# An attention stage whose softmax, weight conversion and matmuls are put in another order

## The chip, the cores and the metric

One core of a Trainium2 chip runs the whole kernel. A core has TensorE (PE: matmuls; PEld in the profile is its weight load), VectorE (DVE), ScalarE (ACT), GpSimd (POOL) and SyncE (SP, whose queue issues most DMAs). Each engine works through its own instructions in order and waits for others by semaphores. The time is that of one execution on the device in microseconds (us), the median of several.

## The reference

A trunk of two layers over 256 tokens of width 1024, all in float32. The stage that is edited is the attention of layer 1: three head groups of eight heads of 64, each with its own causal window and dilation; keys and values `k_sh`, `v_sh` are computed before.

```python
q = apply_rope((h @ w_q).reshape(B, S, N_ATTN_GROUPS, HEADS_PER_GROUP, HEAD_DIM), cos, sin)
for g, (window, dilation) in enumerate(ATTN_GROUPS):     # per group
    s = einsum(q, k) * Dh ** -0.5;  s = where(mask, s, NEG_BIG)
    m = max(s);  p = exp(s - m);  den = sum(p)
    o = einsum(p / den, v);  lse = m + log(den)
wts = softmax(stack(lses), axis=0)                       # over the groups
o = sum(wts[..., None] * stack(outs), axis=0)
return o.reshape(B, S, O_WIDTH) @ w_o
```

Weighting the groups by their `lse` and adding them is one softmax over the keys of all three groups together, which is how the kernel does it. After the mixer come a post norm, the residual sum, a pre norm and a SwiGLU feed-forward.

## The kernel before

**Numbers in two parts.** For matmuls each float32 weight is split: `hl[:, 0]` is the weight rounded to a shorter form (the high part, a copy on ScalarE, L99), `hl[:, 1]` what is left (the low part, a subtraction on VectorE, L100). Activations are split alike. A product is three matmuls (`proj_mm`, `row_mm`): high by high, high by low, low by high. Weights come by DMA in blocks into three raw buffers (`rawp`) and are converted into `hl` buffers (six, and two more called `xy`). A DMA waits on SP's queue until the block that had its raw buffer is converted.

**Tiles.** The tokens are two halves of 128 (`i` = 0, 1). The heads are eight in each group, two at a time: four pairs (`pr` = 0 to 3), with all three groups of the pair together, 384 query columns. So there are eight half tiles `(pr, i)`.

**A half tile** takes these steps:
- `q_proj`: 24 matmuls into a PSUM bank `qp`, in two halves of 12, with weights of `load_q_units`.
- `rope` (the rotation): four VectorE instructions (L658 to L662, `ra_q`, `rb_q`).
- `q_turn`: three transposes on PE into `qtp`, copied by ScalarE to `qT` (L772).
- `scores`: 12 matmuls into two PSUM banks `sc` (one for each head, `e` = 0, 1); VectorE adds the mask and takes the row maximum (L710), multiplies it by -0.125 (`nm`, L712), ScalarE takes the exponential and its row sum `den` (L714).
- `over_sums`: VectorE's reciprocal (L720), and GpSimd's multiplication of the weights `p` by it (L721).
- `p_turn`: eight transposes on PE into `ptp`, two ScalarE copies (L737).
- `values`: 16 matmuls into `ob`; ScalarE and VectorE split the result into the parts of `oT` (L748, L749).

**The tail.** `o_proj(i, chunks)` multiplies `oT` by the output weights, one of four chunks for each pair, into two banks `acc_o` of each half. `go.first` is the post norm with the residual sum, `go.second` the pre norm, `go.third` the transposes `tp_m` into the next input `aT`; `go(1, ...)` does all three for half 1. The next feed-forward opens with the matmuls `acc_b`, whose first four converted blocks it takes from `first_units` if there are any, or loads.

**What sets the order.** The kernel's tool decides the order of instructions on each engine by itself, except within `manual_schedule`, where the engines that it names go in the order in which the code is written. In the loop over pairs that holds for PE, VectorE and ScalarE, in the tail for PE alone. PSUM banks are handed round: four for `qp`, `sc` and `acc_o`, two (`gu`) for `qtp`, `ob` and the last scores, two for `ptp` and `tp_m`; a step waits until the user of its bank before has been read.

Of the kernel before, what the change touches and what calls it, by code (L numbers as in the profile page):

```python
# [19 lines left out]
P = 128  # L20
# [27 lines left out]
def trunk_kernel(ctx: ExitStack, tc: tile.TileContext, x, pos, gains, pscale, ws, wq, invf, amask, pmat, icnt, out):  # L48
# [72 lines left out]
    def load_q_units(pr, b):  # L121
        raw = rawp.tile([P, 2, 1024], F32, tag="raw", name=f"rawq{pr}{b}")
        nc.sync.dma_start(raw[:, :, :768], wq[pr * 2 + b])
        return [parts(raw, k, 768, pr % 2 == 0 and b == 0) for k in range(2)]
# [564 lines left out]
    qT = [qx[g // 2][:, g % 2].rearrange("p (r s) -> p r s", r=4) for g in range(3)]  # L689
    am = qx[2][:, 0].bitcast(BF16).rearrange("p (i k) -> p i k", i=2)  # L690
    pTt = [t.rearrange("p (c t) -> p c t", c=4) for t in (qx[1][:, 1, 0:512], qx[1][:, 1, 512:1024], qx[2][:, 1])]
    nc.gpsimd.dma_start(am, amask.rearrange("i p k -> p i k"))
    npt = [0]
    probs = {}

    def scores(pr, i, pool=accp, tag="acc"):
# [3 lines left out]
        sc = [pool.tile([P, 512], F32, tag=tag, name=f"sc{i}_{pr}{e}") for e in range(2)]  # L700
        for o, g, keys in ((0, 0, slice(0, S)), (256, 1, t), (384, 2, t)):
            for e in range(2):
                a = slice(e * 64, e * 64 + 64)
                n = keys.stop - keys.start
                mm(sc[e][:, o : o + n], q[g][a, t], kT[g][a, pr, keys], True, True)
        probs[i, pr] = []
        for e in range(2):
            p = sc2.tile([P, 512], F32, tag="w2", name=f"p{i}_{pr}{e}")
            mx = st.tile([P, 1], F32, tag="mx", name=f"mx{i}_{pr}{e}")
            nc.vector.tensor_tensor_reduce(p, sc[e], am[:, i], 1.0, -3.0e38, op0=ALU.add, op1=ALU.max, accum_out=mx)  # L710
            nm = st.tile([P, 1], F32, tag="nm", name=f"nm{i}_{pr}{e}")
            nc.vector.tensor_scalar_mul(nm, mx, -0.125)  # L712
            den = st.tile([P, 1], F32, tag="den", name=f"den{i}_{pr}{e}")
            nc.scalar.activation(p, p, AF.Exp, bias=nm, scale=0.125, accum_out=den)  # L714
            probs[i, pr].append((p, den))

    def over_sums(pr, i):
        for e, (p, den) in enumerate(probs[i, pr]):
            rd = st.tile([P, 1], F32, tag="rd", name=f"rd{i}_{pr}{e}")
            nc.vector.reciprocal(rd, den)  # L720
            nc.gpsimd.tensor_scalar_mul(p, p, rd)  # L721
            probs[i, pr][e] = p

    oT = [None, None]

    pT = {}

    def p_turn(pr, i):

        pT[i, pr] = []  # L730
        for e in range(2):
            tp = tpp.tile([P, 4, P], F32, tag="tp", name=f"ptp{i}_{pr}{e}")
            for c in range(4):
                nc.tensor.transpose(tp[:, c], probs[i, pr][e][:, c * P : (c + 1) * P], ident)
            pT[i, pr].append(pTt[npt[0] % len(pTt)])
            npt[0] += 1
            nc.scalar.copy(pT[i, pr][e], tp)  # L737

    def values(pr, i):
# [4 lines left out]
        for c, (g, j) in enumerate(((0, 0), (0, 1), (1, i), (2, i))):  # L744
            for e in range(2):
                n = slice((2 * pr + e) * 64, (2 * pr + e) * 64 + 64)
                mm(ob[e * 64 : e * 64 + 64, 0:P], vt[g][:, j, n], pT[i, pr][e][:, c], c == 0, c == 3)
# [3 lines left out]
    acc_f = [None, None]  # L751

    def o_proj(i, chunks):
# [5 lines left out]
    def q_proj(pr, i, half, units):  # L759
# [4 lines left out]
        if half == 1:  # L764
            qr[pr, i] = rope(qp[i][:, :384], i, 6, f"q{pr}{i}")

    def q_turn(pr, i):
# [3 lines left out]
        for g in range(3):  # L771
            nc.scalar.copy(qT[g][:, pr, i * P : (i + 1) * P], tp[:, g])  # L772

    qp, qr = {}, {}
    units = []

    def next_q(pr, k):

        if k % 2 == 0:
            units.extend(load_q_units(pr + 1, k // 2) if pr < 3 else load_units(2))  # L780

    with tc.manual_schedule(engines={mybir.EngineType.PE}):
        with tc.manual_schedule(engines={mybir.EngineType.DVE, mybir.EngineType.Activation}):
# [178 lines left out]
```

## Time and profile before

| | |
|---|---|
| median of 3 runs (lowest, highest) | 984.6 us (982.15, 986.87) |
| the profiled execution, its span | 985.76 us, 984.0 us |
| mean granted clock of PE | 0.986 |
| busy: PE, PEld, VectorE, ScalarE, GpSimd | 950.4, 783.7, 684.1, 542.9, 62.3 us |
| first query matmul of the stage | 699.35 us |
| first matmul of the output projection | 767.43 us |
| gate matmuls of the last feed-forward run on from | 794.77 us |

The span runs from the first to the last instruction; the execution's time is some 2 us longer. Matmuls overlap at their ends, so paces are read from start to start. A row of the trace's order of time has the start, the length, the engine, the line, the operation with what it writes and reads, how many were merged, and in brackets how long the engine had waited before it and for whom. The "granted clock" is the share of PE's full clock.

### The profile page before, as it was taken

What the parts mean: (1) busy time and instruction counts of PE and PEld (TensorE: products, weight loads), DVE (VectorE), ACT (ScalarE), POOL (GpSimd) and SP (SyncE); (2) the same over time, 40 slices, a digit from 0 to 9 for tenths busy, and PEclk for the clock granted to TensorE, in tenths of its full rate; (3) what the DMA queues carried; (4) which work ended last, traced back from release to release, by engine and by line L of the source; (5) the groups of instructions that cost most, each with busy time, mean ns of one, the idle gap of its engine ahead of it and who ended that gap; (6) DMA issues with size and microseconds to landing.
All of it is one profiled execution on the core that took longest, in us unless ns stands there. A gap on an engine that the chain in (4) does not pass through costs nothing.

```text
span 984.0 us, 12092 instructions
## 1 busy us (share of the span) xinstructions
PE 950.4 (97%) x4560; PEld 783.7 (80%) x4560; DVE 684.1 (70%) x771; ACT 542.9 (55%) x693; POOL 62.3 (6%) x66
## 2 busy tenths in 40 slices
PE   7999999999999999999999999999987899999997
PEld 6888788878788878877888888788976778887886
DVE  5979874577788886458887964785465587887642
ACT  6665753455657565347656743644345576665531
POOL 0000000000100000000000000100033310000000
PEclk8999999999999999999999999999999799999999
DMA  7886876475468687546687765564324236967721
GB/s 248 286 266 205 259 260 207 173 227 187 164 211 265 181 280 261 179 139 213 153 317 218 268 243 175 177 217 139 127 95 153 86 107 194 330 163 260 247 90 43
DMA packets 55898, 197.16 MB, mean 200 GB/s; under 512 B 7392, under 2 KB 7392, under 8 KB 53792
## 3 DMA queue, kind: packets, MB, share of 16 engines
q1 hardware_dynamic: 53456, 179.35, 52.2%
q0 software_dynamic: 2384, 17.04, 8.9%
q8 instruction: 36, 0.59, 0.2%
q14 instruction: 22, 0.18, 0.0%
HBM read 178.54 MB, written 1.05 MB: 183 GB/s over the span
## 4 chain that ended last, share of the span: by engine, by line
PE 74%; DVE 11%; ACT 5%; DMA 4%; issue 3%; POOL 2%; SPq 0%; POOLq 0%; DVEq 0%; ACTq 0%
PE acc_d L127 22%; PE g L127 12%; PE st L314 12%; PE u L127 7%; PE acc_b L127 6%; PE vp L127 3%; DVE hl L100 3%; PE kp L127 3%; DMA xy<-raw 2%; DVE hl_lo L107 2%; PE htp L295 2%; ACT hl L99 2%; PE qp L127 1%; DVE h L193 1%; PE acc_w L127 1%
## 5 line engine op out<-in xcount | busy, mean ns | idle before, releaser
L100 DVE TENSOR_TENSOR hl<-raw,hl 128x1024 fp32r<-128x1024 f32 x182 | 221.0, 1222 | 111.6 <-ACT hl L99 110.5
L99 ACT CAST hl<-raw 128x1024 fp32r<-128x1024 f32 x182 | 189.7, 1051 | 138.3 <-PE acc_d L127 103.3
L127 PE MATMUL acc_d<-hl,h 128*128 128x512 f32 x1056 | 243.5, 390 | 0.0
L127 PEld LDWEIGHTS acc_d<-hl,h 128*128 128x128 f32 x1056 | 197.3, 188 | 40.4
L107 DVE TENSOR_TENSOR hl_lo<-xy,hl_hi 128x2048 fp32r<-128x2048 f32 x40 | 91.6, 2291 | 48.6 <-ACT hl_hi L106 48.6
L107 DVE TENSOR_TENSOR hl_lo<-raw,hl_hi 128x2048 fp32r<-128x2048 f32 x48 | 109.4, 2285 | 15.6 <-ACT hl_hi L106 15.5
L106 ACT CAST hl_hi<-xy 128x2048 fp32r<-128x2048 f32 x40 | 76.5, 1913 | 64.0 <-DVE xy L333 29.7
L106 ACT CAST hl_hi<-raw 128x2048 fp32r<-128x2048 f32 x48 | 91.9, 1914 | 20.8 <-PE st L314 10.6
L127 PE MATMUL acc_b<-hl,aT_m 128*128 128x512 f32 x192 | 44.8, 392 | 0.3 <-ACT aT_m L205 0.3
L127 PEld LDWEIGHTS acc_b<-hl,aT_m 128*128 128x128 f32 x192 | 35.7, 188 | 8.3 <-ACT aT_m L205 0.8
L127 PE MATMUL g<-hl_hi,aT_m 128*128 128x512 f32 x128 | 41.9, 393 | 0.0
L127 PE MATMUL u<-hl_hi,aT_m 128*128 128x512 f32 x128 | 41.8, 393 | 0.0
L314 PE MATMUL st<-hl_hi,S_m 128*128 128x512 f32 x128 | 41.8, 393 | 0.0
L127 PE MATMUL qp<-hl,aT_f 128*128 128x384 f32 x192 | 38.9, 354 | 0.0
L297 ACT CAST h<-htp 128x512 fp32r<-128x512 f32 (+1 forms) x48 | 26.2, 548 | 20.0 <-PE htp L295 20.0
L127 PEld LDWEIGHTS qp<-hl,aT_f 128*128 128x128 f32 x192 | 34.8, 198 | 1.3 <-issue 0.8
L127 PE MATMUL kp<-hl,aT_hk 128*128 128x512 f32 x144 | 34.6, 394 | 0.0
L331 POOL DMA_DIRECT2D xy<-raw x16 | 14.1, 878 | 305.2 <-DVE xy L333 82.3
L127 PE MATMUL vp<-hl,aT_hk 128*128 128x512 f32 x144 | 33.1, 390 | 0.0
L314 PE MATMUL st<-hl_hi,aT_m 128*128 128x512 f32 x96 | 31.6, 393 | 1.3 <-ACT hl L99 0.9
L721 POOL TENSOR_SCALAR p<-p,rd 128x512 f32<-128x512 f32 x16 | 24.9, 1566 | 121.9 <-DVE rd L720 100.1
L298 DVE TENSOR_TENSOR h<-htp,h 128x512 fp32r<-128x512 f32 (+1 forms) x48 | 30.6, 640 | 1.1 <-ACT h L297 1.0
(246 smaller groups left out, 1596.4 us busy)
## 6 DMA issues: line engine op xcount, KB each, us to landing
raw<-in_ws SPq DMA_DIRECT2D x278, 512.0 KB, 4.8
xy<-in_ws SPq DMA_DIRECT2D x32, 512.0 KB, 6.8
xy<-raw POOLq DMA_DIRECT2D x16, 1024.0 KB, 8.1
rawq<-in_wq SPq DMA_DIRECT2D x8, 768.0 KB, 4.7
gain_post<-in_gains SPq DMA_DIRECT2D x14, 256.0 KB, 5.0
gain_pre<-in_gains SPq DMA_DIRECT2D x12, 256.0 KB, 6.1
rawpm<-in_pmat SPq DMA_DIRECT2D x2, 512.0 KB, 4.1
out_dram<-h SPq DMA_DIRECT2D x4, 256.0 KB, 2.1
```

What stands on the lines that cost most here:

```text
L99: nc.scalar.copy(hl[:, 0, :n], raw[:, k, :n])
L100: last["dve"] = nc.vector.tensor_sub(hl[:, 1, :n], raw[:, k, :n], hl[:, 0, :n])
L106: nc.scalar.copy(hi, raw)
L107: last["dve"] = nc.vector.tensor_sub(lo, raw, hi)
L127: nc.tensor.matmul(o, l, r, start=start, stop=stop)
L193: nc.vector.scalar_tensor_tensor(h[i][:, c], y[:, c], rs, h[i][:, c], op0=ALU.mult, op1=ALU.add)
L295: nc.tensor.transpose(tp[:, k], prod[c, i][:, k * P : (k + 1) * P], ident)
L297: nc.scalar.copy(d[:, 0], tp[:, :nt])
L298: nc.vector.tensor_sub(d[:, 1], tp[:, :nt], d[:, 0])
L314: nc.tensor.matmul(ps, a(z, k), u[v], start=start and k == 0 and n == 0, stop=k == 3 and n == 2, skip_group_check=not start,)
L331: nc.gpsimd.dma_start(dst, src, accum_op=ALU.add)
L721: nc.gpsimd.tensor_scalar_mul(p, p, rd)
```

## The change

The loop's steps are written anew in half-tile steps. One function, `between`, stands after each half tile's query matmuls. It does the high parts of one block of weights, issues the next block's DMA, then the rotation of this half tile, scores and masks of the half tile before (`new`), the transposes and copies of the softmax weights of the one before that (`old`), with the exponentials around the copies, then the low parts, and last the division by the sums. Transposes of the queries and value matmuls stand between the two halves of the next 12 query matmuls. Besides:
- the weights `p` are divided by their sums on VectorE, not on GpSimd;
- the mask instruction scales by -0.125 and takes the minimum, so the separate small multiplication goes;
- three query copies become two; the buffers of turned softmax weights are two, not three;
- blocks of output weights go through `between` too (`b` = 8, 9), and two blocks of first gate weights are converted by hand in the tail;
- the tail's order is written anew, and holds for VectorE and ScalarE as well.

```diff
-            nc.vector.tensor_tensor_reduce(p, sc[e], am[:, i], 1.0, -3.0e38, op0=ALU.add, op1=ALU.max, accum_out=mx)
-            nc.vector.tensor_scalar_mul(nm, mx, -0.125)
-            nc.scalar.activation(p, p, AF.Exp, bias=nm, scale=0.125, accum_out=den)
+        nc.vector.tensor_tensor_reduce(
+            p, sc[pr, i][e], am[:, i], -0.125, 3.0e38, op0=ALU.add, op1=ALU.min, accum_out=nm
+        )
+        nc.scalar.activation(p, p, AF.Exp, bias=nm, scale=-1.0, accum_out=den)
...
-            nc.gpsimd.tensor_scalar_mul(p, p, rd)
+        nc.vector.tensor_scalar_mul(p, p, rd)
...
+    def between(b, q, new, old):
+        z = high(b)
+        if b < 9:
+            next_raw(b + 1)
+        q_rope(*q)
+        if new is not None:
+            score_mm(*new)
+            for e in range(2):
+                masked(*new, e)
+        if old is not None:
+            p_turn(*old)
+        if new is not None:
+            exped(*new, 0)
+        if old is not None:
+            for e in range(2):
+                p_copy(*old, e)
+        if new is not None:
+            exped(*new, 1)
+        u = low(z)
+        if new is not None:
+            for e in range(2):
+                over_sum(*new, e)
+        return u
...
+            q_proj(pr, 0, 0, cur)
+            if pr > 0:
+                q_turn(pr - 1, 1)
+            if pr > 1:
+                value_mm(pr - 2, 1)
+            q_proj(pr, 0, 1, cur)
+            units += between(2 * pr + 2, (pr, 0), (pr - 1, 1) if pr > 0 else None, (pr - 1, 0) if pr > 0 else None)
...
+        raw = load_raw()
+        first_units += [parts(raw, k, xy=True) for k in range(2)]
+        o_proj(0, 0, 1)
+        q_turn(3, 1)
+        value_mm(2, 1)
+        raw = load_raw()
+        o_proj(0, 2)
+        score_mm(3, 1, gup, "gu")
...
+        o_proj(0, 3)
         go.first(0, acc_f[0])
+        p_turn(3, 1)
+        p_copy(3, 1, 0)
+        p_copy(3, 1, 1)
+        o_proj(1, 2)
+        value_mm(3, 1)
         go.second(0)
+        o_proj(1, 3)
     go.third(0)
```

**VectorE in the loop**, around the half tile `(2, 0)`, before. A name such as `p_10` is half, pair and head of the softmax weights; `nm` is its column for the exponential, `hl` converted weights, `ISA` the mask instruction with its reading of the accumulator.

```order
L720 RECIPROCAL rd_11_5737<-den_11_5719 128x1 [waits Activation_49]
L100 TENSOR_TENSOR hl<-rawq_5759,hl 128x768 [waits DMAHW7_49,Activation_49]
L100 TENSOR_TENSOR hl<-rawq_5759,hl 128x768 [waits Activation_49]
L658 TENSOR_TENSOR ra_q_5779<-qp_5721,ctab 128x384 [waits PE_49]
L661 TENSOR_TENSOR rb_q_5780<-qp_5721,stab 128x6x32 x2
L662 TENSOR_TENSOR ra_q_5779<-ra_q_5779,rb_q_5780 128x384 [waits DVE_49]
L710 ISA p_10_5793,mx_10_5794<-sc_10_5785,qT_5420 128x512 [waits PE_49]
```

After:

```order
L658 TENSOR_TENSOR ra_q_5773<-qp_5724,ctab 128x384 [waits PE_49]
L661 TENSOR_TENSOR rb_q_5774<-qp_5724,stab 128x6x32 x2
L662 TENSOR_TENSOR ra_q_5773<-ra_q_5773,rb_q_5774 128x384 [waits DVE_49]
L714 ISA p_10_5787,nm_10_5788<-sc_10_5779,qT_5420 128x512 [waits PE_49]
L714 ISA nm_10_5788 128x1
L714 ISA p_11_5790,nm_11_5791<-sc_11_5780,qT_5420 128x512 [waits PE_49]
L714 ISA nm_11_5791 128x1
L795 TENSOR_TENSOR hl<-rawq_5678,hl 128x768 [waits DMAHW7_49,Activation_49]
L795 TENSOR_TENSOR hl<-rawq_5678,hl 128x768 [waits Activation_49]
L728 RECIPROCAL rd_10_5811<-den_10_5803 128x1 [waits Activation_49]
L729 TENSOR_SCALAR p_10_5787<-p_10_5787,rd_10_5811 128x512 [waits DVE_49]
```

The low parts (L100 before, L795 after) stood ahead of the rotation and masks, and now stand behind them, ahead of the division.

**ScalarE at the start of the tail**, before (`raw_6063` is the second block of output weights, `raw_6394` one of gate weights, `qtp_6127` the last transposed queries):

```order
L99 CAST hl<-raw_6063 128x1024 [waits DMAHW4_49]
L99 CAST hl<-raw_6394 128x1024 [waits DMAHW7_49,PE_49]
L99 CAST hl<-raw_6394 128x1024 [waits DMAHW0_49,PE_49]
L772 COPY qT_5418<-qtp_6127 128x128 [waits PE_49]
L772 COPY qT_5418<-qtp_6127 128x128
L772 COPY qT_5419<-qtp_6127 128x128
L714 ACTIVATE p_30_6098,den_30_6103<-p_30_6098,nm_30_6101 128x512 [waits DVE_49,Pool_49]
```

After (`raw_6093` is the first block of gate weights):

```order
L722 ACTIVATE p_30_6063,den_30_6079<-p_30_6063,nm_30_6064 128x512 [waits DVE_49]
L740 COPY qT_5419<-ptp_20_6069 128x512 [waits PE_49,Activation_49]
L740 COPY qT_5419<-ptp_21_6074 128x512 [waits PE_49,Activation_49]
L722 ACTIVATE p_31_6066,den_31_6083<-p_31_6066,nm_31_6067 128x512 [waits DVE_49]
L99 CAST hl<-raw_6093 128x1024 [waits DMAHW5_49]
L99 CAST hl<-raw_6093 128x1024 [waits DMAHW6_49]
L774 COPY qT_5418<-qtp_6116 128x2x128 [waits PE_49]
L775 COPY qT_5419<-qtp_6116 128x128
L751 CAST oT_5743<-ob_2_6122 128x128 [waits PE_49]
```

Exponentials and copies of the pair 3's first half and pair 2's second, and two conversions, now stand ahead of the last query copies.

**PE at the same place**, after (`acc_o` are sums of the output projection, `sc_30` and `sc_31` the last scores):

```order
L772 MATMUL qtp_6116<-ident,ra_q_6049 128x128 x2
L127 MATMUL ob_2_6122<-qT_5419,kv_4930 64x128 [waits Activation_49] x2
L127 MATMUL ob_2_6122<-qT_5419,kv_4930 64x128 x2
L127 MATMUL ob_2_6122<-qT_5419,kv_4931 64x128 x4
L127 MATMUL acc_o_6102<-hl,oT_5650 128x512
L127 MATMUL acc_o_6103<-hl,oT_5650 128x512
L127 MATMUL acc_o_6102<-hl,oT_5650 128x512 [waits DVE_49]
L127 MATMUL acc_o_6103<-hl,oT_5650 128x512
L127 MATMUL acc_o_6102<-hl,oT_5650 128x512
L127 MATMUL acc_o_6103<-hl,oT_5650 128x512
L127 MATMUL sc_30_6142<-kv_4929,qT_5418 128x256 [waits PE_49,Activation_49]
L127 MATMUL sc_31_6143<-kv_4929,qT_5418 128x256 [waits DVE_49]
```

Before, the scores stood behind weight transposes and had other banks to wait for:

```order
L734 MATMUL ptp_30_6146<-ident,p_30_6098 128x128 [waits Pool_49]
L734 MATMUL ptp_30_6146<-ident,p_30_6098 128x128 x3
L734 MATMUL ptp_31_6152<-ident,p_31_6105 128x128 [waits Pool_49]
L734 MATMUL ptp_31_6152<-ident,p_31_6105 128x128 x3
L127 MATMUL sc_30_6158<-kv_4929,qT_5418 128x256 [waits Activation_49]
L127 MATMUL sc_31_6159<-kv_4929,qT_5418 128x256 [waits Activation_49]
```

Values of pair 2's second half now stand ahead of the last scores and use one of their two banks (`ob_2`), and the wait for GpSimd is gone from this place.

More of the change, by code (lines that the diff above doesn't have):

```diff
@@ L733, in p_turn, with p_copy, value_mm @@
             for c in range(4):
[L734 to L739, printed above, removed]
+                nc.tensor.transpose(tp[:, c], probs[pr, i, e][0][:, c * P : (c + 1) * P], ident)
+            pT[pr, i, e] = tp
+    def p_copy(pr, i, e):
+        nc.scalar.copy(pTt[e], pT[pr, i, e])
+    def value_mm(pr, i):
         if oT[i] is None:
```

151 lines of the change are left out of this document (72 added, 79 removed).

## The prediction

> **What bounds the kernel now.** I read the page first (which engine is full), then the waits and 4 us windows of the attention stage, then the order of time around one wait.
>
> ```profile
> PE 950.4 (97%) x4560; PEld 783.7 (80%) x4560; DVE 684.1 (70%) x771; ACT 542.9 (55%) x693; POOL 62.3 (6%) x66
> ```
>
> TensorE (PE) has 33.6 us without a matmul in the whole span of 984.0 us. A third of that lies in the stage that is edited. In windows of 4 us from 696 to 800 us (columns: length, then busy us of PE, PEld, DVE, ACT, POOL, then granted clock, DMA share, GB/s):
>
> ```profile
> 760.00:764.00 4.00, 3.75 (x20) 3.22 (x21) 0.47 (x5) 2.44 (x8) 3.11 (x2) 0.50 0.37 149
> ...
> 776.00:780.00 4.00, 3.12 (x23) 2.68 (x24) 1.50 (x6) 1.09 (x2) 0.00 (x0) 0.50 0.02 4
> ...
> sum 104.00, PE 92.93 PEld 79.94 DVE 62.76 ACT 56.90 POOL 27.49; mean PE 3.57 PEld 3.07 DVE 2.41 ACT 2.19 POOL 1.06
> ```
>
> Idle: 104.00 - 92.93 = 11.1 us. The second loss is inside "busy": in windows behind waits the granted clock falls to 0.50. What PE waits for (us in total, times, longest):
>
> ```profile
> PE ob L127 <- ACT qT L737: 6.1, 3, 2.6
> PE ptp L734 <- POOL p L721: 2.7, 3, 1.3
> ```
>
> `ob` are the value matmuls, which need the copies of the turned softmax weights out of PSUM (L737); `ptp` turn the weights, which POOL has divided by their sums. Two short waits, then one long one with what leads to it, in order of time:
>
> ```profile
> 721.43 2.46 PE L127 MATMUL ob<-qT,kv 128*64 128x128 f32 x16 [2.22 <-ACT qT L737]
> ...
> 740.12 1.58 PE L127 MATMUL ob<-qT,kv 128*64 128x128 f32 x16 [1.27 <-ACT qT L737]
> ...
> 755.32 1.22 DVE L100 TENSOR_TENSOR hl<-raw,hl 128x1024 fp32r<-128x1024 f32 x1
> ...
> 757.06 0.55 PE L770 MATMUL qtp<-ident,ra_q 128*128 128x128 f32 x3 [1.17 <-DVE ra_q L662]
> ...
> 757.84 0.72 ACT L714 ACTIVATE p<-p,nm 128x512 f32<-128x512 f32 x1 [3.93 <-DVE nm L712]
> ...
> 760.25 2.46 PE L127 MATMUL ob<-qT,kv 128*64 128x128 f32 x16 [2.65 <-ACT qT L737]
> ...
> 762.64 3.78 PE L127 MATMUL qp<-hl,aT_f 128*128 128x384 f32 x12
> ```
>
> VectorE makes low parts of weights (L100) in the middle of the rotation. The rotation, mask and exponentials are late, the copies stand behind the exponentials on ScalarE, and PE sits 2.65 us. After it the 16 value matmuls take 2.46 us.
>
> PE's unhindered pace:
>
> ```profile
> 743.94 1.15 PE L127 MATMUL sc<-kv,qT 64*128 64x256 f32 x12
> 745.01 2.35 PE L127 MATMUL qp<-hl,aT_f 128*128 128x384 f32 x12
> 747.21 0.49 PE L770 MATMUL qtp<-ident,ra_q 128*128 128x128 f32 x3
> 747.53 1.04 PE L734 MATMUL ptp<-ident,p 128*128 128x128 f32 x8
> 748.32 2.35 PE L127 MATMUL qp<-hl,aT_f 128*128 128x384 f32 x12
> 750.61 1.15 PE L127 MATMUL sc<-kv,qT 64*128 64x256 f32 x12
> 751.68 1.09 PE L127 MATMUL ob<-qT,kv 128*64 128x128 f32 x16
> 752.71 1.09 PE L734 MATMUL ptp<-ident,p 128*128 128x128 f32 x8
> ```
>
> From start to start: scores 1.07, 12 query matmuls 2.20 to 2.29 (I use 2.25), query transposes 0.32, weight transposes 0.79 (I use 0.8), values 1.03. So the wait of 2.65 us was followed by a loss of 1.4 us in the values and 1.4 in the next 12 query matmuls; the wait of 2.2 us by the same 1.4 in the values, that of 1.3 us by 0.5.
>
> The stage's limits are these starts:
>
> ```profile
> 699.35 6.43 PE L127 MATMUL qp<-hl,aT_f 128*128 128x384 f32 x36
> ...
> 767.43 1.66 PE L127 MATMUL acc_o<-hl,oT 128*128 128x512 f32 x6
> ...
> 784.08 0.60 ACT L174 ACTIVATE jk_pm<-acc_o 128x512 bf16<-128x512 f32 x1 [0.59 <-PE acc_o L127]
> ...
> 791.67 0.98 PE L203 MATMUL tp_m<-ident,n_m 128*128 128x128 f32 x7
> ...
> 794.77 1.53 PE L127 MATMUL acc_b<-hl,aT_m 128*128 128x512 f32 x6
> ```
>
> The loop takes 767.43 - 699.35 = 68.1 us. Its work at full pace: 16 x 2.25 + 7 x 1.07 + 7 x 0.32 + 5 x 0.8 + 5 x 1.03 = 54.9. So 13.2 us are lost there. The tail (output projection and first half of the boundary) takes 27.3 us to 794.77.
>
> **The change, part by part.** Durations (line, engine, operation, count | busy, mean ns of one):
>
> ```profile
> L721 POOL TENSOR_SCALAR p<-p,rd 128x512 f32<-128x512 f32 x16 | 24.9, 1566 | 121.9 <-DVE rd L720 100.1 <-ACT qT L737 15.0 <-PE qtp L770 6.9
> ...
> L100 DVE TENSOR_TENSOR hl<-raw,hl 128x1024 fp32r<-128x1024 f32 x11 | 13.3, 1221 | 3.4 <-ACT hl L99 3.4
> ...
> L99 ACT CAST hl<-raw 128x1024 fp32r<-128x1024 f32 x12 | 12.3, 1054 | 0.7 <-PE qp L127 0.4 <-PE acc_o L127 0.2
> L714 ACT ACTIVATE p<-p,nm 128x512 f32<-128x512 f32 x16 | 11.5, 722 | 24.9 <-DVE nm L712 24.8
> L100 DVE TENSOR_TENSOR hl<-rawq,hl 128x768 fp32r<-128x768 f32 x12 | 11.5, 991 | 11.8 <-ACT hl L99 11.8
> L710 DVE CUSTOM_DVE_ANT_0 p<-sc,qT 128x512 f32<-128x512 f32 x16 | 10.9, 685 | 5.6 <-PE sc L127 5.3 <-issue 0.3
> ...
> L737 ACT COPY qT<-ptp 128x512 f32<-128x512 f32 x16 | 8.8, 592 | 4.1 <-PE ptp L734 4.1
> ...
> L714 ACT ACTIVATION_READ_ACCUMULATOR p<-p,nm 128x1 f32 x16 | 3.0, 186 | 0.0
> ...
> L720 DVE RECIPROCAL rd<-den 128x1 f32<-128x1 f32 x16 | 2.4, 160 | 4.3 <-ACT p L714 3.8
> ...
> L256 DVE TENSOR_SCALAR n_m<-n_m,rs_qm 128x512 f32<-128x512 f32 x1 | 0.5, 487 | 0.4 <-POOL rs_qm L178 0.4
> ```
>
> *Normalising on VectorE.* It leaves POOL (2 x 1.57 us per half tile, one after the other) and costs VectorE 2 x (0.16 + 0.49) = 1.3 us. The 0.49 is another line's multiply of the same shape by a column. *Mask with minimum and factor -0.125.* That form isn't in the trace. Same shape, so 0.685; half of it or double are the ends, 0.7 us per step either way on VectorE. Its separate small multiply (L712) goes. *Query copies 3 to 2*: I count 0 for it, since ScalarE isn't late there (below); were it late, one short copy would be the gain.
>
> *Order of a half tile.* The rotation's four instructions, with nothing between, go from 744.52 to 746.19, 1.7 us:
>
> ```profile
> 744.52 0.55 DVE L658 TENSOR_TENSOR ra_q<-qp,ctab 128x384 f32<-128x384 f32 x1
> ...
> 745.63 0.56 DVE L662 TENSOR_TENSOR ra_q<-ra_q,rb_q 128x384 f32<-128x384 f32 x1
> ```
>
> Take zero at the end of its last query matmul.
> - PE: scores to 1.1, weight transposes of the half before to 1.9, the next 12 query matmuls to 4.15, query transposes to 4.5, values to 5.5, 12 query matmuls to 7.75. That is the step.
> - VectorE: rotation to 1.7, two masks to 3.2, two low parts to 5.2, two normalisations to 6.5: 6.5 of 7.75 us, 6.8 with the small subtraction behind the values. It isn't the bound, but near.
> - ScalarE: first exponential from 2.45 (first mask done) to 3.35 with its accumulator read, two copies to 4.5, second exponential to 5.4, then query copies, `oT`, and the weights' high parts for the next step.
> - The value matmuls want the copies at 4.5 and get them at 4.5: margin nil. The turned weights are wanted 8.8 after the mask's zero and normalised at 6.5: margin 2.3. The low parts, done by 5.2, are wanted at 5.5 by the next 12 query matmuls: margin 0.3.
>
> So the waits of the loop go, except for small ones where the margin is nil: between 0 and 0.5 us in each of six steps; I take 1.0 in all, near the lower end since the copies overlap somewhat. One weight transpose group moves from the tail into the loop (0.8). Loop: 54.9 + 0.8 + 1.0 = 56.7, a gain of 11.4 us. The weights' DMAs are issued one step ahead into the same three buffers; what must be free was converted two steps earlier, so SP's queue isn't late. POOL's queue holds only the mask's load, long done.
>
> *The tail gets new waits.* The four converted tiles of the first gate weights (L99, L100, 1.05 and 1.22 us each) all fall into it; two were in the loop before. Six projection matmuls take 1.5 us at full pace:
>
> ```profile
> 786.58 1.66 PE L127 MATMUL acc_o<-hl,oT 128*128 128x512 f32 x6
> 788.08 1.04 PE L734 MATMUL ptp<-ident,p 128*128 128x128 f32 x8
> ```
>
> Same zero, at the last half tile:
> - The conversions stand ahead of the last query copy on ScalarE (5.4 + 2.1, copy done 8.1) and of the subtraction that frees the bank of `ob` on VectorE (weights' low parts of 1024 columns to 5.7, normalising to 7.0, conversions to 9.4, subtraction to 9.7). PE has projected chunks 0, 1 and 2, with query transposes and values between, by 1.9 + 4.5 + 0.3 + 1.0 = 7.7 and can start the last scores at 8.1, but their second bank only at 9.7: 2 us of wait.
> - Then masks, exponential, copies: values of half 0 at 13.4 instead of 12.9 (0.5), the cast of their result behind two more conversions (0.7), the last copies behind two conversions and two squares (0.7).
> - The first half's sum is complete at 18.5. Its chain to the first transposes took 791.67 - 784.08 = 7.6 us before; with a conversion more on each side I take 8.9, so 27.4. PE has 4.9 us of work and 1 us of waits meanwhile: idle from 24.2 to 27.4, 3.2 us.
> - The gate matmuls run on at 28.5, thus 26.6 after the loop's end (1.9).
>
> Before it was 27.3 less 0.4 for two gate matmuls already done: 26.9. At full clock the tail is a draw (-0.3).
>
> *The clock.* The waits of 2.2 and 2.65 us cost at least 1.4 and 2.8 us after them (above). Of my two gaps I charge 1.0 to the first, since scores lie inside it, and 2.0 to the second: 3.0. Ends: 0 and 6.
>
> The Trainium skill ("TensorE: Matmul & The Clock Gate", Part 1) lets the clock fall to half after about 3.4 us of idleness and rise after as much work. The values at 721.43, at half pace after a wait of 2.2 us, don't fit that if all work counts. By that rule the first gap would cost nothing, and the sum would be 1 us lower.
>
> Sum: -11.4 - 0.3 + 3.0 = -8.7. Against the profiled execution (985.76 us, span 984.0): 977.1. The median of the runs is 1.2 us lower, so 975.9 there; I say 976.0. A change under 0.5% (4.9 us) can't be told from none.
>
> **Rivals.**
> 1. *The clock holds in the tail.* Mechanism: only gaps without any matmul for longer than those two halve the clock. For it: the wait of 1.3 us at 738.9 us was followed by an almost undisturbed pace. Against: 2.2 us did it. Time 976.0 - 3 = 973.0. (It is the skill's rule, carried to both gaps.) Chance 0.22.
> 2. *No change to tell.* The clock stays at half from the last scores to the first half's sum, 9.7 to 18.5: 0.9 + 0.8 + 4.5 + 1.0 = 7.2 us of PE work double, 1.2 of it into waits that are there anyway. With 1.0 already charged that is +5.0, so 981.0. For it: the window 776 to 780 at 0.50 shows such a stretch in the same place. Chance 0.20.
> 3. *Slower.* Place: the value matmuls, whose margin is nil. The path from query matmul over rotation, mask, exponential and two copies to the values, and on through 12 query matmuls, is itself 7.75 us. If it is longer by e, PE waits e in each of six steps, and from about 1 us on the clock falls as well (0.7 us more each). At e = 0.75, 6 x 1.45 = 8.7 us eats the gain; a mask that takes double (two of them, 1.4) would give 976.0 + 6 x 2.1 = 988.6. Against: every piece but the mask has a row. Chance 0.10.
>
> **How the numbers follow.** Forecast 976.0 has 0.48 (974.5 to 979.7). Range: down to 971 (rival 1 with the loop's small waits at nothing and a shorter boundary chain), up to 982 (rival 2). Left out: most of rival 3, the edges of 1 and 2, under 0.2. Faster: forecast and rival 1, 0.70; same 0.20; slower 0.10.
>
> **What would show it.** Right: the value and weight-transpose waits gone or under 0.5 us each, granted clock 1.00 over the loop, 56 to 58 us from the first query matmul to the first of the output projection; a wait of the last scores of about 2 us, put down to VectorE's subtraction or ScalarE's copy; some 3 us ahead of the boundary's first transposes with a clock below 1 behind it. Wrong: values still waiting over 1 us per step (rival 3), no lowered window in the tail (rival 1), or a mask instruction away from 0.685 us.

## The result and the profile after

The changed kernel takes 971.72 us (median of 4 runs, 970.61 to 972.27). The kernel before, on the same chip, takes 985.12 us. The ratio is 0.9866 (95% interval 0.9849 to 0.9884), so 13.4 us are gained. Forecast were 976.0 us, with 971 to 982 as range: the time lies at the range's lower edge, and the gain is about half as large again as the 8.6 us forecast.

The line of the engines on the page of the changed kernel (span 968.8 us):

```profile
PE 945.6 (98%) x4560; PEld 779.2 (80%) x4560; DVE 687.3 (71%) x771; ACT 540.8 (56%) x685; POOL 37.3 (4%) x50
```

What PE waits for between 695 and 800 us (us in total, times, longest). The value matmuls `ob` and the weights' transposes `ptp`, which led this list before, are gone:

```profile
PE tp_m L203 <- DVE n_m L256: 2.4, 1, 2.4
PE sc L127 <- DVE oT L752: 0.5, 1, 0.5
PE acc_o L127 <- ACT oT L751: 0.4, 1, 0.4
PE acc_o L127 <- DVE oT L752: 0.3, 1, 0.3
```

The 4 us windows from 696 to 800 us (same columns as before): the clock is 1.00 in every window up to 776 us and is lowered in two. Idle are 104.00 - 100.36 = 3.6 us, against 11.1.

```profile
776.00:780.00 4.00, 2.32 (x9) 2.07 (x10) 2.93 (x7) 2.87 (x6) 1.56 (x2) 0.70 0.05 19
780.00:784.00 4.00, 4.00 (x17) 3.21 (x16) 3.84 (x8) 2.77 (x7) 0.36 (x1) 0.88 0.00 0
...
sum 104.00, PE 100.36 PEld 85.78 DVE 76.95 ACT 64.56 POOL 4.09; mean PE 3.86 PEld 3.30 DVE 2.96 ACT 2.48 POOL 0.16
```

PE's order of time, with the stage's start, one half-tile step in the middle, and the tail's limits:

```profile
698.31 6.43 PE L127 MATMUL qp<-hl,aT_f 128*128 128x384 f32 x36
...
729.95 1.09 PE L736 MATMUL ptp<-ident,p 128*128 128x128 f32 x8
...
733.39 1.09 PE L127 MATMUL ob<-qT,kv 128*64 128x128 f32 x16
...
737.80 1.09 PE L736 MATMUL ptp<-ident,p 128*128 128x128 f32 x8
...
754.36 3.01 PE L127 MATMUL acc_o<-hl,oT 128*128 128x512 f32 x12
...
761.42 1.14 PE L127 MATMUL sc<-kv,qT 64*128 64x256 f32 x10 [0.47 <-DVE oT L752]
...
773.60 1.65 PE L127 MATMUL acc_o<-hl,oT 128*128 128x512 f32 x6 [0.35 <-ACT oT L751]
777.68 1.94 PE L203 MATMUL tp_m<-ident,n_m 128*128 128x128 f32 x8 [2.43 <-DVE n_m L256]
779.44 6.70 PE L127 MATMUL acc_b<-hl,aT_m 128*128 128x512 f32 x25
```

A step takes 737.80 - 729.95 = 7.85 us without a wait. The loop takes 754.36 - 698.31 = 56.05 us (68.1 before), the tail to the gate matmuls 779.44 - 754.36 = 25.1 us (27.3 before). That is 12.0 and 2.2 us. The spans differ by 15.2 us; the missing us is that the stage starts 1.04 us earlier in this execution, before any edited line.

### The profile page after: what moved, and what is told of

Same layout as the page of the kernel before. It is cut to its first block, busy times and chain, and to the rows that moved or that the text cites. A ratio compares the mean times of both kernels' runs of the same rounds, so it can differ in the third digit from the quotient of the medians.

```text
span 968.8 us, 12052 instructions
## 1 busy us (share of the span) xinstructions
PE 945.6 (98%) x4560; PEld 779.2 (80%) x4560; DVE 687.3 (71%) x771; ACT 540.8 (56%) x685; POOL 37.3 (4%) x50
## 3 DMA queue, kind: packets, MB, share of 16 engines
HBM read 178.54 MB, written 1.05 MB: 185 GB/s over the span
## 4 chain that ended last, share of the span: by engine, by line
PE 80%; DVE 10%; issue 3%; ACT 3%; DMA 2%; POOL 2%; SPq 0%; POOLq 0%; DVEq 0%; ACTq 0%
PE acc_d L127 22%; PE st L314 12%; PE g L127 12%; PE u L127 7%; PE acc_b L127 7%; PE qp L127 4%; PE vp L127 3%; PE kp L127 3%; DVE hl L100 2%; DVE hl_lo L107 2%; PE htp L295 2%; PE acc_w L127 1%; PE acc_u L127 1%; DVE h L193 1%; DMA xy<-raw 1%
## 5 line engine op out<-in xcount | busy, mean ns | idle before, releaser
L100 DVE TENSOR_TENSOR hl<-raw,hl 128x1024 fp32r<-128x1024 f32 x178 | 216.1, 1221 | 108.4 <-ACT hl L99 107.3
L99 ACT CAST hl<-raw 128x1024 fp32r<-128x1024 f32 x178 | 185.5, 1051 | 139.4 <-PE acc_d L127 103.2
L106 ACT CAST hl_hi<-raw 128x2048 fp32r<-128x2048 f32 x48 | 91.8, 1913 | 24.1 <-PE st L314 10.6
L127 PEld LDWEIGHTS vp<-hl,aT_hk 128*128 128x128 f32 x144 | 27.0, 188 | 5.6
L127 PEld LDWEIGHTS kp<-hl,aT_hk 128*128 128x128 f32 x144 | 26.6, 188 | 5.4
```

The costliest lines, as they stand in the source:

```text
L99: nc.scalar.copy(hl[:, 0, :n], raw[:, k, :n])
L100: last["dve"] = nc.vector.tensor_sub(hl[:, 1, :n], raw[:, k, :n], hl[:, 0, :n])
L106: nc.scalar.copy(hi, raw)
L127: nc.tensor.matmul(o, l, r, start=start, stop=stop)
```

## The experiments

The main theory, A in the expectations: the loop's gain comes from the order. In the old order the conversion of the next weights stands ahead of the rotation, mask and exponentials, these are late, the copies behind them on ScalarE are late, and the value matmuls wait. The first rival is the division: GpSimd's 1.57 us per instruction would be what made the weights, and the values behind them, late. The other letters are explained in the expectation that uses them. Each ratio is against runs of the kernel before on the same chip. No run takes by themselves the factor folded into the mask, the two query copies, the smaller number of buffers, or the new places of PE's transposes and values.

**The changed kernel, division back on GpSimd.**

```diff
-        nc.vector.tensor_scalar_mul(p, p, rd)
+        nc.gpsimd.tensor_scalar_mul(p, p, rd)
```

> The new order, but GpSimd divides the weights by their sums as before (1.57 us each, two in a row). Theory A (the order of the conversions carried the loop's gain): no wait in the loop, since in the changed kernel's trace the sums' reciprocals are ready at 733.5 and the transposes want the weights at 737.8, and two divisions of 1.57 fit into that; VectorE gets 1.0 us per step free. Loop 56 to 57 us, whole time within 2 us of the changed kernel's 971.7. Theory B (the slow division on GpSimd carried it): weight transposes wait for GpSimd again, 0.5 us or more in each step, 5 us or more lost, 977 or above.

Measured: 971.45 us, ratio 0.9873 (0.9858 to 0.9888), the same as the changed kernel. On GpSimd the instruction takes 1.64 us instead of 0.487 on VectorE, and PE notices one wait for it between 695 and 800 us:

```profile
L729 POOL TENSOR_SCALAR p<-p,rd 128x512 f32<-128x512 f32 x16 | 26.1, 1640 | 105.8 <-DVE rd L728 105.8
...
PE ptp L736 <- POOL p L729: 0.4, 1, 0.4
```

In the new order the place of the division is worth nothing that the times show: the division has half a step and more before the transposes want it.

**The changed kernel, low parts back ahead of the rotation.**

```diff
         z = high(b)
         if b < 9:
             next_raw(b + 1)
+        u = low(z)
         q_rope(*q)
...
-        u = low(z)
```

> The new kernel with one thing put back: the low parts of the weights stand ahead of the rotation. Theory A: the round from values over oT, the high parts, the second low part, rotation, mask, exponential and two copies to the next values closes on itself: 1.05 + 0.3 + 1.6 + 0.95 + 1.65 + 0.65 + 0.15 + 0.9 + 1.05 = 8.3 us against PE's 7.85, so 0.45 us of wait at the values in each of six steps, 3 us in all, 974 to 976. Theory B: the same time as the changed kernel, 971 to 972.5.

Measured: 974.45 us, ratio 0.9903 (0.9886 to 0.9919), so about 3 us are given back. The loop takes 699.53 to 758.51 = 59.0 us instead of 56.05, and the old wait is back in small:

```profile
PE ob L127 <- ACT qT L740: 1.5, 2, 1.1
```

The time is the one that theory A gave, the place only in part: it expected 0.45 us of wait in each of six steps. From one group of values to the next the steps take 8.04 to 8.52 us instead of 7.85; the list shows two waits, and the rest is in rows of values that have grown from 1.09 to between 1.31 and 1.57 us.

The order of the low parts is a true part of the gain. It is a quarter of the 12 us. That the high parts are early here and late in the old order would explain why it is no more; this was not tried by itself in the new order.

**The kernel before, division on VectorE.**

```diff
-            nc.gpsimd.tensor_scalar_mul(p, p, rd)
+            nc.vector.tensor_scalar_mul(p, p, rd)
```

> The kernel before with one part of the change alone: VectorE divides the weights by their sums. Theory A: the waits for GpSimd go (2.7 us, nearly all in the tail), the waits at the values stay; 0 to 3 us faster than before, 982 to 985. Theory B: more than half of the change's gain, 978 or below.

Measured: 979.08 us, ratio 0.9949 (0.9934 to 0.9964), 4.7 us faster, between the theories. In the profile the loop is only 1.8 us shorter (698.14 to 764.42, 66.3 us): the values wait almost as before, which the division can't help. The tail is 3.5 us shorter (764.42 to 788.25, 23.8 us): there the last weights are wanted at once, and the wait for GpSimd was real. With it goes a lowered clock: the windows from 776 to 784 us stood at 0.50 and 0.64 before, and are at 1.00 here.

```profile
PE ob L127 <- ACT qT L737: 5.6, 3, 2.5
```

**The kernel before, the whole conversion behind the scores.** High and low parts together are moved.

```diff
-                next_q(pr, 0)
                 q_proj(pr, 0, 1, cur)
                 if pr > 0:
                     scores(pr - 1, 1)
+                next_q(pr, 0)
...
-                next_q(pr, 2)
                 q_proj(pr, 1, 1, cur)
                 scores(pr, 0)
+                next_q(pr, 2)
```

> The kernel before with one part of the change alone: the weights' conversions (high and low parts together) stand behind the scores, masks and exponentials. Theory A: most of the loop's loss goes, 6 to 10 us faster than before, 975 to 979, values hardly wait. Theory B: 0 to 2 us faster. What could spoil A here: high parts come late too, since they move along.

Measured: 985.97 us, ratio 1.0018 (1.0004 to 1.0033): the expectation of theory A missed. One wait was turned into another. ScalarE's high parts now stand behind the exponentials too, so the next query matmuls wait for both parts of their weights, and the values still wait:

```profile
PE ob L127 <- ACT qT L772: 6.4, 2, 4.7
PE qp L127 <- ACT hl L99: 2.2, 3, 1.2
PE qp L127 <- DVE hl L100: 1.6, 3, 0.6
...
757.74 1.05 ACT L99 CAST hl<-raw 128x1024 fp32r<-128x1024 f32 x1 [4.30 <-DMA raw<-in_ws]
```

The last line is part of the longest wait, 4.7 us, and has to do with something else: ScalarE stands 4.30 us for the DMA of a block of weights, ahead of both exponentials, where the written order has no conversion. By its place this is a tile of the first gate weights, which the tool put there; the next run shows the same. Without this wait the run might have gained something, but the 3.8 us of waits for both parts of the weights would still be there. So moving the whole conversion is not enough for the 6 to 10 us expected. The theory had to be sharper: the low parts behind the softmax, the high parts where they were.

**The kernel before, only the low parts behind the scores.**

```diff
-                next_q(pr, 0)
+                z = high_q(pr, 0)
                 q_proj(pr, 0, 1, cur)
                 if pr > 0:
                     scores(pr - 1, 1)
+                low_q(z)
...
-                next_q(pr, 2)
+                z = high_q(pr, 1)
                 q_proj(pr, 1, 1, cur)
                 scores(pr, 0)
-                next_q(pr, 3)
+                low_q(z)
```

> The kernel before, with the conversions cut in two: high parts on ScalarE where they were, low parts on VectorE behind the scores and masks; GpSimd still divides. The run that moved both parts behind the softmax gained nothing, its values waited for ScalarE. Theory A (what counts is that the low parts let rotation and masks through, while the high parts stay early): 4 to 8 us faster than before, 976 to 980, waits of the values cut by half or more. Theory C (the old places of the turns and values, next to the steps that make their input, hold the waits whatever VectorE's order): within 2 us of the kernel before.

Measured: 982.27 us, ratio 0.9974 (0.9962 to 0.9987), 3 us faster where 5 and more were expected. The loop does what theory A says: it takes 698.54 to 761.19 = 62.7 us, 5.4 less, and almost without a wait until one of 4.25 us at its end. In the tail 3 us are given back (761.19 to 791.50, 30.3 us). The waits for GpSimd are not what is new there: they are 2.7 us in all, as before. New are a wait of 1.3 us for a low part and a longer stretch of lowered clock (0.74, 0.50, 0.50 and 0.98 in the four windows from 768 to 784 us). What makes the one wait in the loop, on ScalarE and VectorE:

```profile
747.65 1.05 ACT L99 CAST hl<-raw 128x1024 fp32r<-128x1024 f32 x1 [2.06 <-DMA raw<-in_ws]
748.73 1.22 DVE L100 TENSOR_TENSOR hl<-raw,hl 128x1024 fp32r<-128x1024 f32 x1 [1.78 <-ACT hl L99]
...
749.88 0.15 DVE L712 TENSOR_SCALAR nm<-mx 128x1 f32<-128x1 f32 x1
...
751.92 0.72 ACT L714 ACTIVATE p<-p,nm 128x512 f32<-128x512 f32 x1 [1.05 <-DVE nm L712]
...
754.42 1.97 PE L127 MATMUL ob<-qT,kv 128*64 128x128 f32 x16 [4.25 <-ACT qT L772]
...
PE ptp L734 <- POOL p L721: 2.7, 3, 1.7
```

The two tiles of the first gate block (L99, L100; the output weights have other lines in this run) are not written in the loop. The tool puts them there, ScalarE waits 2.06 us for their DMA ahead of the exponentials, and VectorE makes a low part (748.73) between the mask and the small multiplication (749.88) that the exponential needs. The changed kernel writes these conversions at a place of its own in the tail.

The same holds for the longest wait that the prediction showed of the kernel before. The low part at 755.32, in the middle of the rotation, is a gate tile too: the rotation is written without a break, and the two low parts written ahead of it stand at 752.05. So that wait has two causes, the order of the loop and the tool's tiles in it, and the prediction took them for one.

**The same, and the division on VectorE.**

> The kernel before with the low parts of the query weights behind the scores and masks (as in the run that split high and low parts) and, besides, the division on VectorE. Theory A (order and division are two prices that add where each has its own wait): the three waits of the weights' transposes for GpSimd, 2.7 us in all, go, and the tail comes back from 30.3 us towards the 23.8 that the division alone gave; the one wait of the values behind the gate weights' low parts stays, about 4 us. 977 to 979.5 us. Rival F (once the loop is on time, the division is hidden wherever it is done, and the tail's 30.3 us come from the order of the conversions): 981 to 983 us, the waits for GpSimd replaced by others of the same size.

Measured: 975.65 us, ratio 0.9911 (0.9888 to 0.9935). The two parts give 4.7 and 3.0 us alone and 9.0 together: they add, within the interval. The waits for the division fall from 2.7 to 0.5 us, and the tail is at full clock from 760 us on. The loop takes 697.39 to 758.89 = 61.5 us, the tail 24.8. What still parts this kernel from the changed one (4.4 us by the ratios, 5.45 us in the loop) is, in its trace, the wait at the gate blocks and the slow matmuls behind it:

```profile
751.74 1.98 PE L127 MATMUL ob<-qT,kv 128*64 128x128 f32 x16 [2.73 <-ACT qT L772]
753.65 4.21 PE L127 MATMUL qp<-hl,aT_f 128*128 128x384 f32 x12
```

By the full pace of the prediction (1.03 and 2.25 from start to start), that is 2.7 + (753.65 - 751.74 - 1.03) + (757.79 - 753.65 - 2.25) = 5.5 us, where 757.79 is the start of the next scores. That taking away this wait alone would give the changed kernel's time was not tried; the run that gives the changed kernel's tail back to the tool, below, puts such a wait in.

**The changed kernel, the mask delayed by two instructions.** VectorE does two more additions ahead of the first mask of each half tile but the last; their result is overwritten. This asks how much room the values have, which the prediction called nil.

```diff
+        if e == 0 and (pr, i) != (3, 1):
+            for _ in range(2):
+                nc.vector.tensor_add(p, sc[pr, i][e], am[:, i])
```

> The changed kernel with two extra VectorE additions of scores and mask (about 0.65 us each from start to start) ahead of the first mask of each half tile but the last; their result is overwritten. In the changed kernel's trace the second copy of the turned weights ends 0.3 us before the values start, so a delay of 1.3 us should show as 1.0 us of wait in each of six steps. Theory D (only the wait counts): 6 us slower than the changed kernel, 977 to 979, clock still 1.00. Theory E (the clock falls too, as the prediction's slower rival had it, 0.7 us more each): 980 to 983. If margin is larger than the trace shows: under 3 us slower.

Measured: 979.44 us, ratio 0.9947 (0.9925 to 0.9968). All five groups of values in the loop wait:

```profile
742.94 1.41 DVE L716 TENSOR_TENSOR p<-sc,qT 128x512 f32<-128x512 f32 x2
744.38 0.69 DVE L717 CUSTOM_DVE_ANT_0 p<-sc,qT 128x512 f32<-128x512 f32 x1
...
745.84 1.05 ACT L743 COPY qT<-ptp 128x512 f32<-128x512 f32 x2
746.46 1.58 PE L127 MATMUL ob<-qT,kv 128*64 128x128 f32 x16 [0.63 <-ACT qT L743]
...
746.94 0.85 PEld L127 LDWEIGHTS ob<-qT,kv 128*64 128x64 f32 x14 [0.30 <-ACT qT L743]
...
755.47 1.57 PE L127 MATMUL ob<-qT,kv 128*64 128x128 f32 x16 [0.63 <-ACT qT L743]
```

The delay is 744.38 - 742.94 = 1.44 us, the step 755.47 - 746.46 = 9.01 instead of 7.85: 1.16 of 1.44 reach PE, so the room is 0.28 us. Of the 1.16, the list of waits shows 0.63. The rest is inside the row of 1.58: the matmuls begin after the first copy, and behind the first two of them PE waits for the second copy, which ends at 746.89 (the weight loads go on at 746.94). The time is 0.4 us above the range of theory D and below that of E; the clock is 1.00 through the loop, as D has it. What D left out is a wait of 1.5 us, once, for low parts that the two additions delay as well.

**The same with one instruction.**

> The changed kernel with one extra VectorE addition ahead of the first mask of each half tile (its result is overwritten), so a delay of about 0.72 us. Theory D (the values have a margin of 0.3 us behind the copies and the rest is waited for): 0.72 less 0.3 = 0.4 us in each of six steps, the step 8.25 us instead of 7.85, 973.5 to 975 us. Theory G (any wait has a further fixed price in the value matmuls, of about 0.5 us): the step 8.75 us, 976 to 978 us. Theory H (the margin is larger than the trace's 0.3 us, the two-fold delay was partly hidden): under 972.5 us.

Measured: 975.04 us, ratio 0.9905 (0.9884 to 0.9927). Here the list of waits shows nothing for the values, and yet the loop is 2.9 us longer (699.20 to 758.16). Only the length of the row and the step tell it:

```profile
735.91 1.55 PE L127 MATMUL ob<-qT,kv 128*64 128x128 f32 x16
744.19 1.55 PE L127 MATMUL ob<-qT,kv 128*64 128x128 f32 x16
```

A step is 744.19 - 735.91 = 8.28 us, 0.43 more for a delay of about 0.72: the room is again 0.29 us. Two delays, one straight line: theory D. The time lies just above the upper end of its range, 975; the low parts are also late once (a wait of 0.7 us for `hl`), which D had left out.

**The changed kernel, the tail's order given back to the tool** for VectorE and ScalarE.

```diff
+    with tc.manual_schedule(engines={mybir.EngineType.PE}):
         raw = load_raw()
         first_units += [parts(raw, k, xy=True) for k in range(2)]
```

> The changed kernel, but in the tail only PE keeps the written order; VectorE and ScalarE are placed by the tool, as before the change. If the hand order of VectorE and ScalarE in the tail costs time (conversions ahead of what PE waits for): 1 to 2 us faster than the changed kernel, 970 to 971, the 2.4 us wait of the boundary's first transposes shorter. If it doesn't matter: within 1 us of 971.7.

Measured: 971.52 us, ratio 0.9866 (0.9839 to 0.9892): no difference. The tool shortens the boundary's wait and holds up the loop's last values for it:

```profile
PE tp_m L203 <- DVE n_m L256: 1.6, 1, 1.6
PE ob L127 <- ACT qT L740: 1.2, 1, 1.2
...
745.28 1.05 ACT L99 CAST hl<-raw 128x1024 fp32r<-128x1024 f32 x1 [1.04 <-DMA raw<-in_ws]
746.37 1.23 DVE L100 TENSOR_TENSOR hl<-raw,hl 128x1024 fp32r<-128x1024 f32 x1 [0.91 <-ACT hl L99]
```

Two differences of nearly the same size stand behind the equal times. The tool puts the first gate block into the loop again: the low part at 746.37 stands ahead of the rotation's last instruction (747.51), and the values at 750.04 wait. The loop takes 697.99 to 755.76 = 57.8 us, 1.7 longer. In return the tail, without these tiles, takes 755.76 to 778.12 = 22.4 us, 2.7 shorter, at full clock. So the gate tiles cost the loop time in the new order as well, which bears out the reading of the two runs with split conversion.

**The changed kernel with a tail in another order.** The gate weights' tiles are spread singly, each where PE has work for the next us; the first half's last chunk is projected as early as its `oT` allows, and the second half's projections are kept to cover the boundary.

```diff
-        first_units += [parts(raw, k, xy=True) for k in range(2)]
+        first_units.append(parts(raw, 0, xy=True))
         o_proj(0, 0, 1)
         q_turn(3, 1)
         value_mm(2, 1)
+        first_units.append(parts(raw, 1, xy=True))
...
-        first_units += [parts(raw, k) for k in range(2)]
         o_proj(1, 0)
         value_mm(3, 0)
-        o_proj(1, 1)
+        first_units.append(parts(raw, 0))
         o_proj(0, 3)
         go.first(0, acc_f[0])
...
-        o_proj(1, 2)
+        o_proj(1, 1)
         value_mm(3, 1)
+        o_proj(1, 2)
         go.second(0)
         o_proj(1, 3)
-    go.third(0)
+        go.third(0)
+        first_units.append(parts(raw, 1))
```

> The changed kernel with a new tail: the fourth chunk of half 0 is projected directly behind its values, so that its boundary starts 2 us earlier, with two chunks and the values of half 1 behind it to cover the chain, and two of the four conversions of gate weights moved behind what PE waits for. Walked from the changed kernel's rows: sum of half 0 complete at 13.4 us after the loop's end and not 15.6, gate matmuls from 21.7 to 22.7 and not 25.1. No gap of 2 us is left, so the clock stays at 1.00 and the slow 1.7 us go too. 967.0 to 969.5. If the clock falls anyway, or the low part of the last gate tile is late: 970 to 971.5.

Measured: 968.71 us (967.5 to 968.86), ratio 0.9834 (0.9814 to 0.9854). It is the fastest of all. Both the time and the start of the gate matmuls (22.2 us after the loop's end) lie in the ranges expected. The clock stays at 1.00 through the tail, and the boundary's wait is 0.7 instead of 2.4:

```profile
PE tp_m L203 <- DVE n_m L256: 0.7, 1, 0.7
...
755.94 3.01 PE L127 MATMUL acc_o<-hl,oT 128*128 128x512 f32 x12
...
778.13 7.50 PE L127 MATMUL acc_b<-hl,aT_m 128*128 128x512 f32 x31 [0.18 <-DVE aT_m L206]
```

The 3.0 us that it gains (971.72 to 968.71, from two sets of runs, so with some 2 us of uncertainty) agree with the trace, where the tail to the run of gate matmuls is 778.13 - 755.94 = 22.2 us instead of 25.1.

## Why the prediction was right, and where its size was off

- **The loop: right.** Forecast 56.7 us, measured 56.05. The step of 7.75 us came out at 7.85, the waits for values and transposed weights are gone, the clock is 1.00 throughout, the mask instruction takes 0.685 us as before. The mechanism (low parts ahead of rotation, mask and exponentials, hence late copies) is borne out by the run that moves the low parts back and by the one that moves them alone in the old kernel. It is not the whole of the 12.0 us: in the old kernel the low parts bring the loop from 68.1 to 62.7 us and the division brings it to 61.5; the last 5.5 us are, by the traces, the first gate block that the tool had put into the loop. The prediction has that block in its tail, as two more conversions, but not among the reasons for the loop's waits. The run with the tool's tail shows the block's harm in the new order; in the old order no run shows it alone.
- **What the prediction did not see: in every second step the old order is a circle.** Late values make the cast of `oT` late, behind which ScalarE makes the high parts, behind which VectorE makes the low parts, behind which the rotation starts (744.52). In the steps between, the high parts stand behind exponentials and copies. Rows of the kernel before:

```profile
741.74 0.27 ACT L748 CAST oT<-ob 128x128 fp32r<-128x128 f32 x1 [0.68 <-PE ob L127]
741.90 1.57 ACT L99 CAST hl<-rawq 128x768 fp32r<-128x768 f32 x2
742.77 1.83 DVE L100 TENSOR_TENSOR hl<-rawq,hl 128x768 fp32r<-128x768 f32 x2 [0.44 <-ACT hl L99]
```

- **"Margin nil" at the values, charged with 1.0 us: too pessimistic by 0.3 us a step.** Rows below: the exponential starts at 731.30 and the next instruction 0.72 later, not 0.9; both copies take 1.05, not 1.15. They end at 733.07, and the values could start at 733.39. Both delayed runs find the same 0.3 us. Rival 3 thus had its place right, and its threshold 0.3 us further off than stated; the mask, its one unknown, is unchanged. Its further price, a lowered clock from about 1 us of wait a step on, did not come: with 1.16 us a step the clock stayed at 1.00.

```profile
731.30 0.73 ACT L722 ACTIVATE p<-p,nm 128x512 f32<-128x512 f32 x1 [2.89 <-DVE nm L714]
...
732.02 1.05 ACT L740 COPY qT<-ptp 128x512 f32<-128x512 f32 x2
```

- **The tail at full clock, 26.6 us: mis-sized; here and in the clock lies most of the 4.3 us by which the forecast was too slow.** It took 25.1 us with about 1.0 of lowered clock in it (the boundary's eight transposes take 779.44 - 777.68 = 1.76 us, the second half's at full clock 0.79), so some 24.1. "2 us of wait" for the last scores was 1.2: they and what is in them take from 760.25 to 762.49, 2.24 us, where 12 matmuls take 1.07. (The list of waits shows 0.5 of it; the rest is in a row of two matmuls that lasts 0.70 us.) The sum had laid VectorE's instructions end to end by their durations, and they start closer together. Counted from the rotation of the last loop step (752.54), the two low parts are done at 5.2, not 5.7, the conversions at 8.6, not 9.4, and the subtraction that frees the bank at 8.8, not 9.7.

```profile
752.54 0.56 DVE L658 TENSOR_TENSOR ra_q<-qp,ctab 128x384 f32<-128x384 f32 x1 [1.30 <-PE qp L127]
...
755.35 2.35 DVE L795 TENSOR_TENSOR hl<-raw,hl 128x1024 fp32r<-128x1024 f32 x2
...
758.81 2.35 DVE L100 TENSOR_TENSOR hl<-raw,hl 128x1024 fp32r<-128x1024 f32 x2
...
761.08 0.28 DVE L752 TENSOR_TENSOR oT<-ob,oT 128x128 fp32r<-128x128 f32 x1
```

- **The small waits of the tail, 1.9 us in three places, were 0.7 in the list** (0.4 and 0.3 for `oT`, none for the last values).
- **The boundary's gap: right in kind, 2.4 instead of 3.2 us.** (The prediction's own terms, 18.5 + 4.9 + 1, give 24.4 for its start and so 3.0 us.) The chain from the sum to the first transposes took 777.68 - 769.73 = 7.95 us from the first square's start, not 8.9: the conversion that was added on each side did not lengthen it by as much as its own time.
- **The clock, 3.0 us: one of two charges was real.** Behind the last scores the clock did not fall, where PE waited 0.5 us in one piece; behind the boundary it fell, and cost 1.7 us (below; 0.7 of them in the gate matmuls behind the tail) where 2.0 had been charged. Rival 1, "the clock holds in the tail", is half true and names the time better (973.0), for a reason it did not have: the first gap was shorter than forecast, and the second did lower the clock. Of the rule of 3.4 us that the prediction quotes it uses only the first gap's 1.0 us; by that figure both of its gaps, 2 and 3.2 us, would have cost nothing. Rival 2, a tail at half clock throughout, did not come.
- **How near the time came is in part luck.** Profiled execution against profiled execution, 977.1 us were forecast and 970.61 measured. Of these 6.5 us, 5.0 are the tail with its clock (forecast 2.7 us longer than before, measured 2.3 shorter), 0.6 the loop, and 1.0 the stage's earlier start, which no edited line makes. The forecast took off 1.2 us for the median, which lay below the profiled execution before; after, it lies 1.1 us above it. So 4.3 us are left.
- **The division, priced at 1.3 us of VectorE per half tile and no gain of its own: right for this kernel, and not for the one before.** There it is worth 4.7 us, most of it in the tail. The changed kernel can do without it, because its order gives the division time. A part of a change can be worth something alone and nothing in company.

## What to carry to other kernels

Look for instructions that a scheduling tool puts between the written ones: here two conversions for the next stage, among them the low part in the middle of the rotation, stood in the longest wait of the old loop. When an engine converts operands in two parts, place each part by its own consumer: the early part where the next engine can go on from it, the late part behind everything that is on the way to the matmuls. Sum an engine's queue by starts from row to row, not by durations: here a sum of durations put the end of a queue 0.9 us too late. A loop without waits in the list may still lose time, since a merged row that has grown (1.09 to 1.55 us) can hide a wait inside; compare the length of a step as well.

## What was not expected of the hardware

The lowered clock comes in stretches of one length or a multiple of it. The two lowered windows of the changed kernel stand above (0.70 and 0.88). Here are the three of the old kernel with split conversion and VectorE's division, around its wait of 2.73 us:

```profile
748.00:752.00 4.00, 1.27 (x9) 0.99 (x10) 3.96 (x9) 2.87 (x10) 0.00 (x0) 0.88 0.41 108
752.00:756.00 4.00, 4.00 (x23) 3.67 (x22) 1.12 (x4) 2.18 (x4) 0.00 (x0) 0.50 0.95 363
756.00:760.00 4.00, 4.00 (x23) 3.24 (x23) 2.10 (x4) 2.06 (x2) 0.00 (x0) 0.76 0.14 56
```

If the clock is either 1.0 or 0.5, the time at half is twice the missing share: (0.30 + 0.12) x 4 x 2 = 3.4 us in the changed kernel, (0.12 + 0.50 + 0.24) x 4 x 2 = 6.9 us in the other, twice as much. The longest stretch, in the tail of the old kernel with split conversion alone, is three times as long: (0.26 + 0.50 + 0.50 + 0.02) x 4 x 2 = 10.2 us. A fall thus costs a PE that is busy meanwhile 1.7 us, 3.4 or 5.1. The length does not follow the wait ahead of it: a wait of 4.70 us was followed by 3.4 us (the run with the whole conversion moved), one of 2.73 us by 6.9.

The Trainium skill ("TensorE: Matmul & The Clock Gate", Part 1) describes a window of about 3.4 us that runs on freely and in which the gate judges how busy PE is; the lengths of these stretches agree with it. Its rule that an idle gap of more than some 3.4 us is needed does not: the clock fell at every wait of 2.2 us and more (2.22, 2.43 and 2.73 among them), and held after single waits of 1.60 and 1.66 us. Nor does it help to count transposes as idleness: in the changed kernel the last projection matmuls end at 773.60 + 1.65 = 775.25 us, and the clock is at 0.50 from 777.6 us on, 2.3 us later. The waits of 0.6 us in each step of the twice delayed kernel left it at 1.00 through the loop.

That is not a limit for one wait, since the clock also fell behind two shorter waits close together: 1.33 and 0.89 us in the tail of the kernel before (windows from 776 us on), 1.34 and 1.74 us in that of the old kernel with split conversion, and only 0.36 and 1.00 us in that of the twice delayed kernel, at about 770.8 us. How long and how close together waits must be, and how this hangs on where they fall in the window, is open; no run here explains the last of these falls.
